# Opening of a two-layer mixer kernel: products of ones while the input is under way, first weight in halves on ScalarE's queue, blocks of x made straight from PSUM

## Chip, cores and metric

One core of one Trainium2 chip runs the program. The metric is the time of one execution on the device in microseconds (us), the median of several runs.

## What is computed

Two layers of a decoder with four mixing branches, one step for a prompt of 1024 tokens and for 8 single tokens of a second group, which share the weights. Cut to what matters here:

```python
def mixer_layer(x, ...):
    h = rms_norm(x, norm_g)                       # x / sqrt(mean(x^2) + eps) * g
    (a_b, a_c, a_h, a_gate, s_q, s_k, s_v, s_gate,
     c_u, c_v, c_gate, d_q, d_k, d_v, d_gate) = jnp.split(h @ w_in, SPLIT_POINTS, axis=-1)
    k = rope(s_k, pos); q = rope(s_q, pos)        # branch B: attention in a window of 128
    ...                                           # A: short convolution, C: mixing in chunks, D: dilated attention
    merged = sum over n of sigmoid(h @ w_merge[n]) * (branch[n] * silu(gate[n])) @ w_branch[n]
    return x + merged @ w_out
```

The model width is 1024, all arrays are fp32. The opening makes h for all 1032 tokens and the first of these products, the key columns of branch B (S_K).

## The kernel before

A product in fp32 is made of three products of a faster type (fp32r): every operand is split into hi, its rounded value, and lo, the rest, and PE (TensorE) makes hi*hi, hi*lo and lo*hi. For a weight, `w_std` loads the raw tile `wr`, ScalarE (ACT) writes `wh` (line 154) and POOL (GpSimd) subtracts it to get `wl` (line 156). Weight tiles are 128 x 8 x 128: 8 blocks of 128 rows of the model width.

The input x comes with tokens on the partitions and is needed with the width on the partitions. So the opening runs over three groups of token blocks (`GROUPS`: blocks 0 to 2 with the 8 single tokens in front, 3 to 5, 6 and 7), and in each over k = 0 to 7, the blocks of the width. For one k PE transposes the blocks of the group by products with `ident` (lines 259 and 262) into one PSUM tile, `sc` for even k and `ms` for odd k, of which there are two each. DVE (VectorE) copies it to `xT` (line 264), ACT makes `h0h` = hi of x times the norm's gain `gcol` (line 207), and the lo part `h0l` is made by DVE (line 209), or for k = 1 and 5 by ACT (`xg`, line 213) and POOL (line 214). The factor 1 / sqrt(mean) of the norm is applied later, from sums of squares (ACT, line 272, `rtok` at line 320).

Behind the opening `rope_products` multiplies S_K and then the query columns with h in three chunks of 344 tokens (`mm_cols`, lines 178, 181, 182) into `acc` tiles of PSUM, of which there are four.

A list scheduler orders the instructions of every engine; each engine runs its own list in order and waits by semaphores. A transfer is issued on the queue of the engine that the code names: SP (SyncE) for nearly all in the opening. `x` blocks 0 to 2 are loaded in two halves of their columns (`q`), blocks 3 to 7 whole, behind the first weight.

Of the kernel before, what the change touches and what calls it, by code (L numbers as in the profile page):

```python
# [7 lines left out]
F32 = mybir.dt.float32  # L8
F32R = mybir.dt.float32r
AF = mybir.ActivationFunctionType  # L10
# [3 lines left out]
P = 128  # L14
# [18 lines left out]
def kernel(ctx: ExitStack, tc: tile.TileContext, i, o, c):  # L33
# [13 lines left out]
    def slot(name, dt=F32):  # L47
        return sl.tile([P, T], dt, tag="slot", name=name)
# [43 lines left out]
    def load(dst, src, dist):  # L92
        d_ = sp.dma_start(dst, src)
        if len(marks) >= dist:
            tc.add_manual_dep(d_.ins, marks[-dist].name, nosync, reason="prefetch distance")


    ident = cp.tile([P, P], F32, name="ident")
    sp.dma_start(ident, c["ident"])
    band = cp.tile([P, 256], F32, name="band")  # L100
    blk2 = cp.tile([P, P], F32, name="blk2")
    onesm = cp.tile([P, P], F32, name="onesm")
# [46 lines left out]
    def split_w(shape, dmas):  # L149
        raw = wp.tile(list(shape), F32, tag="wr", name="wr", bufs=2)  # L150
        for sel, src in dmas:
            load(sel(raw), src, 4)
        hi = wp.tile(list(shape), F32R, tag="wh", name="wh", bufs=4)
        act.activation(hi, raw, AF.Copy)  # L154
        lo = wp.tile(list(shape), F32R, tag="wl", name="wl", bufs=4)
        pool.tensor_tensor(lo, raw, hi.bitcast(F32), op=ALU.subtract)  # L156
        return hi, lo

    def win_cols(l, c0, n):
# [2 lines left out]
    def w_std(src, kt):  # L162
        r = split_w([P, kt, P], [(lambda t: t, src)])
        copy_piece()
        return r
# [6 lines left out]
        return r  # L172

    def mm_cols(ps, w, kt, xh, xl, cs, first):
        hi, lo = w
        n = cs.stop - cs.start
        for k in range(kt):
            mm = pe.matmul(ps[:, :n], hi[:, k], xh[k][:, cs], start=(k == 0), stop=False)  # L178
            if k == 0 and first:
                mark(mm)  # L180
            pe.matmul(ps[:, :n], hi[:, k], xl[k][:, cs], start=False, stop=False)  # L181
            pe.matmul(ps[:, :n], lo[:, k], xh[k][:, cs], start=False, stop=(k == kt - 1))  # L182

    def mm_chunk(ps, w, kt, xh, xl, ch):
        mm_cols(ps, w, kt, xh, xl, slice(ch * CH, (ch + 1) * CH), kt == KT and ch == 0)
# [41 lines left out]
    def load_x(n0, n1):  # L227
        for n in range(n0, n1):
            xb = slot(f"xin{n}") if n < 5 else dec([P, T], f"xin{n}")
            sp.dma_start(xb[:, :DM], i["x_prompt"][0, n * P:(n + 1) * P, :])  # L230
            xin.append(xb)

    xs = slot("xs")[:NS, :DM]
    for q in range(2):
        fs = slice(q * DM // 2, (q + 1) * DM // 2)
        for n in range(3):
            if q == 0:
                xin.append(slot(f"xin{n}"))
            sp.dma_start(xin[n][:, fs], i["x_prompt"][0, n * P:(n + 1) * P, fs])
            if q == 0 and n == 0:  # L240
                sp.dma_start(xs, i["x_sample"].rearrange("b s d -> (b s) d"))
                sp.dma_start(gcol, i["norm_g"].rearrange("l (k p) -> p l k", p=P))
    w_first = [w_std(win_cols(0, S_K, P), KT)]
    load_x(3, 8)
    fcol = cp.tile([P, KT], F32, name="fcol")
    sp.dma_start(fcol, i["final_norm_g"].rearrange("(k p) -> p k", p=P))
# [4 lines left out]
    for n0, n1 in GROUPS:  # L251
        off = NS if n0 == 0 else 0
        cs = slice(NS + n0 * P - off, NS + n1 * P)
        w = cs.stop - cs.start
        for k in range(KT):
            ks_ = slice(k * P, (k + 1) * P)
            ps = pmisc() if k % 2 else pscore()
            if off:
                pe.transpose(ps[:, 0:NS], xs[:, ks_], ident[:NS, :NS])
            for n in range(n0, n1):  # L260
                c0 = off + (n - n0) * P
                pe.transpose(ps[:, c0:c0 + P], xin[n][:, ks_], ident)
            xt = xT0[k][:, cs]
            dve.tensor_copy(xt, ps[:, :w])
            split_x(0, k, cs, xt, (hh, hl), k % 4 != 1)
    for k in range(KT):
        act.dma_start(xres[0][k], xT0[k])
    sq0 = sm.tile([P, 9], F32, tag="sq0", name="sq0")
# [5 lines left out]
    for l in range(2):  # L274
# [27 lines left out]
            return rope(rope_products([w], [slot(name)])[0])  # L302


        w2 = w_first if l == 0 else [w_std(win_cols(l, S_K, P), KT)]
        w2.append(w_pair(l, S_Q, 0))
        kq = rope_products(w2, [slot("kB"), slot("qB0")])
        cosT, sinT = slot("cosT"), slot("sinT")
# [769 lines left out]
```

## Time and profile before

| what | value |
|---|---|
| median of 3 runs | 2444.82 us (2444.09 to 2446.32) |
| profiled execution | 2436.83 us |
| its span, first to last instruction | 2435.1 us |
| PE busy | 2407.3 us, 99% of the span |
| ACT, DVE, POOL busy | 706.4, 904.7, 846.4 us |
| PE's share of the chain that ended last | 96% |

The profiled execution is one run with its instructions recorded. Its time is 1.73 us more than its span and 7.99 us less than the median. An engine that is busy for 99% of the span leaves 27.8 us in which it stands still.

### The profile page before, as it was taken

What the parts mean: (1) busy time and instruction counts of PE and PEld (TensorE: products, weight loads), DVE (VectorE), ACT (ScalarE), POOL (GpSimd) and SP (SyncE); (2) the same over time, 40 slices, a digit from 0 to 9 for tenths busy, and PEclk for the clock granted to TensorE, in tenths of its full rate; (3) what the DMA queues carried; (4) which work ended last, traced back from release to release, by engine and by line L of the source; (5) the groups of instructions that cost most, each with busy time, mean ns of one, the idle gap of its engine ahead of it and who ended that gap; (6) DMA issues with size and microseconds to landing.
All of it is one profiled execution on the core that took longest, in us unless ns stands there. A gap on an engine that the chain in (4) does not pass through costs nothing.

```text
span 2435.1 us, 38874 instructions
## 1 busy us (share of the span) xinstructions
PE 2407.3 (99%) x15896; PEld 2295.0 (94%) x15896; DVE 904.7 (37%) x1938; ACT 706.4 (29%) x1526; POOL 846.4 (35%) x556
## 2 busy tenths in 40 slices
PE   8999999999999999999999999999999999999999
PEld 7998889889999999999999988898899999999998
DVE  4456534445322122215333554443442221222153
ACT  5234532323212121214323254323222221222243
POOL 3343225342223333444433413353323234434330
PEclk9999999999999999999999999999999999999999
DMA  7242215243321222223442423352352222212232
GB/s 239 90 140 81 81 46 182 66 129 88 106 67 56 96 63 95 66 68 119 148 146 74 143 72 80 89 160 72 90 132 73 70 91 66 93 57 69 76 98 99
DMA packets 295962, 235.82 MB, mean 97 GB/s; under 512 B 52756, under 2 KB 279696, under 8 KB 293416
## 3 DMA queue, kind: packets, MB, share of 16 engines
q1 hardware_dynamic: 267952, 206.25, 28.1%
q10 hardware_dynamic: 27832, 27.10, 3.9%
q8 instruction: 125, 2.05, 0.3%
q14 instruction: 53, 0.43, 0.1%
HBM read 192.35 MB, written 76.47 MB: 110 GB/s over the span
## 4 chain that ended last, share of the span: by engine, by line
PE 96%; DVE 1%; DMA 1%; ACT 1%; POOL 0%; SPq 0%; issue 0%; ACTq 0%; POOLq 0%; DVEq 0%
PE acc L181 27%; PE acc L178 26%; PE acc L182 26%; PE acc L367 2%; PE acc L370 2%; PE acc L371 2%; PE sc L519 2%; PE ms L541 2%; PE ms L536 2%; PE ms L681 1%; DVE ml L902 0%; PE ms L474 0%; POOL qs L291 0%; DMA qs<-dk 0%; DVE dkp L297 0%; PE sc L974 0%
## 5 line engine op out<-in xcount | busy, mean ns | idle before, releaser
L156 POOL TENSOR_TENSOR wl<-wr,wh 128x384 fp32r<-128x384 f32 (+2 forms) x228 | 467.6, 2053 | 846.1 <-ACT wh L154 742.0
L181 PE MATMUL acc<-h0l,wh 128*128 128x344 f32 x1584 | 512.8, 324 | 0.0
L181 PE MATMUL acc<-h1l,wh 128*128 128x344 f32 x1584 | 512.5, 324 | 0.0
L178 PE MATMUL acc<-h0h,wh 128*128 128x344 f32 x1584 | 511.7, 323 | 0.4 <-ACT wh L154 0.3
L178 PE MATMUL acc<-h1h,wh 128*128 128x344 f32 x1584 | 511.7, 323 | 0.1
L182 PE MATMUL acc<-h0h,wl 128*128 128x344 f32 x1584 | 511.4, 323 | 0.0
L182 PE MATMUL acc<-h1h,wl 128*128 128x344 f32 x1584 | 508.7, 321 | 0.0
L154 ACT ACTIVATE wh<-wr 128x384 fp32r<-128x384 f32 (+2 forms) x228 | 205.0, 900 | 428.3 <-PE acc L181 398.2
L937 DVE TENSOR_TENSOR th<-acc,rr 128x344 f32<-128x344 f32 x192 | 99.1, 516 | 567.5 <-PE acc L182 563.9
L181 PEld LDWEIGHTS acc<-h0l,wh 128*128 128x128 f32 x1584 | 299.6, 189 | 9.8 <-issue 8.8
L181 PEld LDWEIGHTS acc<-h1l,wh 128*128 128x128 f32 x1584 | 298.8, 189 | 9.6 <-issue 8.8
L178 PEld LDWEIGHTS acc<-h0h,wh 128*128 128x128 f32 x1584 | 299.6, 189 | 4.4 <-issue 2.0
L178 PEld LDWEIGHTS acc<-h1h,wh 128*128 128x128 f32 x1584 | 298.9, 189 | 3.7 <-issue 2.0
L182 PEld LDWEIGHTS acc<-h0h,wl 128*128 128x128 f32 x1584 | 299.2, 189 | 2.3 <-issue 1.2
L182 PEld LDWEIGHTS acc<-h1h,wl 128*128 128x128 f32 x1584 | 298.7, 189 | 2.3 <-issue 1.2
L943 POOL TENSOR_TENSOR mg<-mg,th 128x344 f32<-128x344 f32 x144 | 138.1, 959 | 309.8 <-DVE th L942 309.8
L938 ACT ACTIVATE th<-th 128x344 f32<-128x344 f32 x192 | 94.3, 491 | 518.7 <-DVE th L937 518.7
L178 PE MATMUL acc<-yh,wh 128*128 128x344 f32 x576 | 184.8, 321 | 0.0
L182 PE MATMUL acc<-yh,wl 128*128 128x344 f32 x576 | 184.8, 321 | 0.0
L181 PE MATMUL acc<-yl,wh 128*128 128x344 f32 x576 | 184.8, 321 | 0.0
L181 PE MATMUL acc<-ml,wh 128*128 128x344 f32 (+3 forms) x384 | 123.1, 322 | 0.6 <-DVE ml L902 0.5
L942 DVE SCALAR_TENSOR_TENSOR th<-th,acc 128x344 f32<-128x344 f32 x144 | 73.9, 513 | 131.5 <-PE acc L182 130.8
(280 smaller groups left out, 3350.3 us busy)
## 6 DMA issues: line engine op xcount, KB each, us to landing
wr<-in_w_merge_dram SPq DMA_DIRECT2D x64, 512.0 KB
out_dram<-in_cache_dil_kv_dram SPq DMA_DIRECT2D x128, 255.9 KB
wr<-in_w_in_dram SPq DMA_DIRECT2D x60, 512.0 KB
y<-yscr SPq DMA_DIRECT2D x18, 516.0 KB
wr<-in_w_branch_dram SPq DMA_DIRECT2D x48, 192.0 KB
wr<-in_w_in_dram SPq DMA_DIRECT2D x32, 256.0 KB
wr<-in_w_out_dram SPq DMA_DIRECT2D x16, 512.0 KB
out_dram<-in_cache_dil_kv_dram SPq DMA_DIRECT2D x16, 511.0 KB
```

The lines of the kernel that those rows point to most:

```text
L154: act.activation(hi, raw, AF.Copy)
L156: pool.tensor_tensor(lo, raw, hi.bitcast(F32), op=ALU.subtract)
L178: mm = pe.matmul(ps[:, :n], hi[:, k], xh[k][:, cs], start=(k == 0), stop=False)
L181: pe.matmul(ps[:, :n], hi[:, k], xl[k][:, cs], start=False, stop=False)
L182: pe.matmul(ps[:, :n], lo[:, k], xh[k][:, cs], start=False, stop=(k == kt - 1))
L367: mm = pe.matmul(ps[:M, :N], lh, hi[:, k % kk], start=(k == 0), stop=False)
L370: pe.matmul(ps[:M, :N], ll, hi[:, k % kk], start=False, stop=False)
L371: pe.matmul(ps[:M, :N], lh, lo[:, k % kk], start=False, stop=(k == KT - 1))
L937: dve.tensor_tensor(t, pg[:, :CH], rr[:, cs], op=ALU.mult)
L938: act.activation(t, t, AF.Tanh, scale=0.5)
L942: dve.scalar_tensor_tensor(t, t, 1.0, pp[:, :CH], op0=ALU.add, op1=ALU.mult)
L943: pool.tensor_tensor(mg[m][:, cs], mg[m][:, cs], t, op=ALU.add)
```

## The change

Five edits, all in the opening:

- `ident`, `xs` (the 8 single tokens) and `gcol` are loaded on ACT's queue in place of SP's.
- The first weight comes as two tiles of 128 x 4 x 128 on ACT's queue, right behind these, in place of one on SP's behind the six halves of x. Each half is split when its `k` is reached; `mm_cols` takes a list of two weights.
- PE multiplies `onesm`, a tile of ones, with itself into a PSUM tile that nothing reads: twelve times ahead of the data, and twice behind the transposes of each of the first four k, 20 in all.
- `split_x` reads the PSUM tile of the transposes, not `xT`. The lo part is made by DVE for every k.
- The copy to `xT` (needed later, for the residual) comes behind it, on DVE for odd k, on ACT for even k.

```diff
-    sp.dma_start(ident, c["ident"])
+    act.dma_start(ident, c["ident"])
...
         raw = wp.tile(list(shape), F32, tag="wr", name="wr", bufs=2)
         for sel, src in dmas:
             load(sel(raw), src, 4)
+        return split_r(shape, raw, pool)
+
+    def split_r(shape, raw, eng):
         hi = wp.tile(list(shape), F32R, tag="wh", name="wh", bufs=4)
         act.activation(hi, raw, AF.Copy)
         lo = wp.tile(list(shape), F32R, tag="wl", name="wl", bufs=4)
-        pool.tensor_tensor(lo, raw, hi.bitcast(F32), op=ALU.subtract)
+        eng.tensor_tensor(lo, raw, hi.bitcast(F32), op=ALU.subtract)
...
         return r
 
     def mm_cols(ps, w, kt, xh, xl, cs, first):
-        hi, lo = w
         n = cs.stop - cs.start
-        for k in range(kt):
-            mm = pe.matmul(ps[:, :n], hi[:, k], xh[k][:, cs], start=(k == 0), stop=False)
-            if k == 0 and first:
+        for k_ in range(kt):
+            (hi, lo), k = (w[k_ // 4], k_ % 4) if isinstance(w, list) else (w, k_)
+            mm = pe.matmul(ps[:, :n], hi[:, k], xh[k_][:, cs], start=(k_ == 0), stop=False)
+            if k_ == 0 and first:
                 mark(mm)
...
+
+    def busy(n):
+        for _ in range(n):
+            pe.matmul(idle[:, :P], onesm, onesm, start=True, stop=True)
+
+    idle = pacc()
+    busy(12)
     xs = slot("xs")[:NS, :DM]
+    w_first = []
     for q in range(2):
         fs = slice(q * DM // 2, (q + 1) * DM // 2)
         for n in range(3):
                 xin.append(slot(f"xin{n}"))
             sp.dma_start(xin[n][:, fs], i["x_prompt"][0, n * P:(n + 1) * P, fs])
             if q == 0 and n == 0:
-                sp.dma_start(xs, i["x_sample"].rearrange("b s d -> (b s) d"))
-                sp.dma_start(gcol, i["norm_g"].rearrange("l (k p) -> p l k", p=P))
-    w_first = [w_std(win_cols(0, S_K, P), KT)]
+                act.dma_start(xs, i["x_sample"].rearrange("b s d -> (b s) d"))
+                act.dma_start(gcol, i["norm_g"].rearrange("l (k p) -> p l k", p=P))
+        w0_ = win_cols(0, S_K, P)[:, 4 * q:4 * q + 4]
+        w_first.append(wp.tile([P, 4, P], F32, tag="wr", name="wr", bufs=2))
+        act.dma_start(w_first[q], w0_)
     load_x(3, 8)
     fcol = cp.tile([P, KT], F32, name="fcol")
     sp.dma_start(fcol, i["final_norm_g"].rearrange("(k p) -> p k", p=P))
...
             for n in range(n0, n1):
                 c0 = off + (n - n0) * P
                 pe.transpose(ps[:, c0:c0 + P], xin[n][:, ks_], ident)
+            if off and k < 4:
+                busy(2)
+            if off and k % 4 == 0:
+                w_first[k // 4] = split_r([P, 4, P], w_first[k // 4], pool)
+            split_x(0, k, cs, ps[:, :w], (hh, hl))
             xt = xT0[k][:, cs]
-            dve.tensor_copy(xt, ps[:, :w])
-            split_x(0, k, cs, xt, (hh, hl), k % 4 != 1)
+            if k % 2:
+                dve.tensor_copy(xt, ps[:, :w])
+            else:
+                act.activation(xt, ps[:, :w], AF.Copy)
     for k in range(KT):
         act.dma_start(xres[0][k], xT0[k])
     sq0 = sm.tile([P, 9], F32, tag="sq0", name="sq0")
...
             return rope(rope_products([w], [slot(name)])[0])
 
 
-        w2 = w_first if l == 0 else [w_std(win_cols(l, S_K, P), KT)]
+        w2 = [w_first] if l == 0 else [w_std(win_cols(l, S_K, P), KT)]
         w2.append(w_pair(l, S_Q, 0))
         kq = rope_products(w2, [slot("kB"), slot("qB0")])
         cosT, sinT = slot("cosT"), slot("sinT")
```

The scheduler places the rows anew. The names in the rows are those of above with a tile number. ACT, start of the program, before:

```order
L207 ACT_TABLE_LOAD
L207 ACTIVATE h0h_0_128<-xT0_0_144,gcol_93 128x392
L207 ACTIVATE h0h_1_129<-xT0_1_145,gcol_93 128x392
L213 ACTIVATE xg_167<-xT0_1_145,gcol_93 128x392
L154 ACTIVATE wh_110<-wr_108 128x1024
L207 ACTIVATE h0h_2_130<-xT0_2_146,gcol_93 128x392
L207 ACTIVATE h0h_3_131<-xT0_3_147,gcol_93 128x392
L207 ACTIVATE h0h_4_132<-xT0_4_148,gcol_93 128x392
L207 ACTIVATE h0h_5_133<-xT0_5_149,gcol_93 128x392
```

ACT, start of the program, with the change:

```order
L99 DMA ident_81<-const_ident_dram 128x128
L252 DMA xs_109<-in_x_sample_dram 8x1024
L253 DMA gcol_93<-in_norm_g_dram 128x16x1
L256 DMA wr_118<-in_w_in_dram 128x4x128
L256 DMA wr_123<-in_w_in_dram 128x4x128
L157 ACT_TABLE_LOAD
L157 ACTIVATE wh_170<-wr_118 128x512
L157 ACTIVATE wh_212<-wr_123 128x512
L210 ACTIVATE h0h_0_139<-sc_163,gcol_93 128x392
L285 ACTIVATE xT0_0_155<-sc_163 128x392
L210 ACTIVATE h0h_1_140<-ms_177,gcol_93 128x392
L210 ACTIVATE h0h_2_141<-sc_187,gcol_93 128x392
L285 ACTIVATE xT0_2_157<-sc_187 128x392
```

The five transfers and both casts (`wh`) stand ahead of the first `h0h`, where before only one cast stood between the second and the third; `h0h` reads `sc` or `ms` in place of `xT`, and a copy to `xT` stands behind each even one.

DVE, its first rows before:

```order
L264 COPY xT0_0_144<-sc_152 128x392
L209 SCALAR_TENSOR_TENSOR h0l_0_136<-xT0_0_144,gcol_93,h0h_0_128 128x392
L264 COPY xT0_1_145<-ms_160 128x392
L264 COPY xT0_2_146<-sc_170 128x392
L209 SCALAR_TENSOR_TENSOR h0l_2_138<-xT0_2_146,gcol_93,h0h_2_130 128x392
L264 COPY xT0_3_147<-ms_178 128x392
L209 SCALAR_TENSOR_TENSOR h0l_3_139<-xT0_3_147,gcol_93,h0h_3_131 128x392
L264 COPY xT0_4_148<-sc_186 128x392
```

and with the change:

```order
L212 SCALAR_TENSOR_TENSOR h0l_0_147<-sc_163,gcol_93,h0h_0_139 128x392
L212 SCALAR_TENSOR_TENSOR h0l_1_148<-ms_177,gcol_93,h0h_1_140 128x392
L283 COPY xT0_1_156<-ms_177 128x392
L212 SCALAR_TENSOR_TENSOR h0l_2_149<-sc_187,gcol_93,h0h_2_141 128x392
L212 SCALAR_TENSOR_TENSOR h0l_3_150<-ms_197,gcol_93,h0h_3_142 128x392
L283 COPY xT0_3_158<-ms_197 128x392
L212 SCALAR_TENSOR_TENSOR h0l_4_151<-sc_207,gcol_93,h0h_4_143 128x392
```

The copy is behind the lo part of its block, and stands there for odd blocks alone.

PE, from the start of the program, before:

```order
L259 MATMUL sc_152<-ident_81,xs_96 128x8
L262 MATMUL sc_152<-ident_81,xin0_97 128x128
L259 MATMUL ms_160<-ident_81,xs_96 128x8
L262 MATMUL ms_160<-ident_81,xin0_97 128x128
L259 MATMUL sc_170<-ident_81,xs_96 128x8
```

and with the change:

```order
L239 MATMUL acc_96<-onesm_85 128x128 x15
L272 MATMUL sc_163<-ident_81,xs_109 128x8
L275 MATMUL sc_163<-ident_81,xin0_110 128x128
L272 MATMUL ms_177<-ident_81,xs_109 128x8
L275 MATMUL ms_177<-ident_81,xin0_110 128x128
L275 MATMUL sc_163<-ident_81,xin1_114 128x128
L275 MATMUL ms_177<-ident_81,xin1_114 128x128
L239 MATMUL acc_96<-onesm_85 128x128
L272 MATMUL sc_187<-ident_81,xs_109 128x8
L275 MATMUL sc_187<-ident_81,xin0_110 128x128
L275 MATMUL sc_187<-ident_81,xin1_114 128x128
L239 MATMUL acc_96<-onesm_85 128x128 x2
```

Fifteen of the twenty products of ones stand ahead of the first transpose, one and two more between the transposes of the third block. The remaining two stand right ahead of the first product with a weight.

## Rows read from the trace of the kernel before

**Rows 1.** The page: busy time, and costliest groups; columns named in the page's text.

```profile
PE 2407.3 (99%) x15896; PEld 2295.0 (94%) x15896; DVE 904.7 (37%) x1938; ACT 706.4 (29%) x1526; POOL 846.4 (35%) x556
...
L937 DVE TENSOR_TENSOR th<-acc,rr 128x344 f32<-128x344 f32 x192 | 99.1, 516 | 567.5 <-PE acc L182 563.9
```

**Rows 2.** Waits of PE, whole program: total us, times, longest us.

```profile
PE ms L501 <- DVE dkp L297: 12.0, 4, 4.7
PE sc L259 <- DMA xs<-in_x_sample_dram: 4.4, 1, 4.4
```

**Rows 3.** Windows: busy us per engine (instructions), granted clock, DMA share, GB/s.

```profile
core 0: us, PE busy (x) PEld busy (x) DVE busy (x) ACT busy (x) POOL busy (x), PEclk, DMA share, GB/s
0.00:5.00 5.00, 0.56 (x2) 0.36 (x2) 0.07 (x1) 0.00 (x0) 0.68 (x9) 1.00 0.53 77
5.00:10.00 5.00, 4.07 (x16) 2.82 (x15) 1.11 (x3) 1.90 (x2) 0.00 (x0) 1.00 0.78 232
10.00:15.00 5.00, 3.92 (x12) 2.34 (x13) 1.03 (x3) 2.67 (x4) 1.42 (x2) 1.00 1.06 378
...
20.00:25.00 5.00, 5.00 (x29) 4.88 (x27) 3.48 (x7) 3.29 (x7) 1.03 (x1) 1.00 0.59 83
25.00:50.00 25.00, 24.98 (x169) 24.24 (x167) 16.53 (x29) 23.91 (x47) 12.70 (x8) 1.00 0.83 292
```

**Rows 4.** Timeline of PE: start, us, line, tiles, [idle before and releaser].

```profile
14.57 0.66 PE L178 MATMUL acc<-h0h,wh 128*128 128x344 f32 x1 [0.29 <-ACT wh L154]
...
17.90 0.27 PE L259 MATMUL ms<-ident,xs 8*128 8x8 f32 x1 [2.39 <-DVE xT L264]
...
19.38 0.49 PE L181 MATMUL acc<-h0l,wh 128*128 128x344 f32 x1
19.66 0.49 PE L182 MATMUL acc<-h0h,wl 128*128 128x344 f32 x1
...
23.37 0.41 PE L178 MATMUL acc<-h0h,wh 128*128 128x344 f32 x1
...
27.43 0.48 PE L178 MATMUL acc<-h0h,wh 128*128 128x344 f32 x2
```

**Rows 5.** Timeline of ACT (ScalarE).

```profile
8.80 0.62 ACT L207 ACTIVATE h0h<-xT,gcol 128x392 fp32r<-128x392 f32 x1 [2.02 <-DVE xT L264]
...
13.46 1.06 ACT L154 ACTIVATE wh<-wr 128x1024 fp32r<-128x1024 f32 x1 [1.74 <-DMA wr<-in_w_in_dram]
...
19.67 0.62 ACT L207 ACTIVATE h0h<-xT,gcol 128x392 fp32r<-128x392 f32 x1 [1.17 <-DVE xT L264]
21.46 0.62 ACT L207 ACTIVATE h0h<-xT,gcol 128x392 fp32r<-128x392 f32 x1 [1.17 <-DVE xT L264]
21.99 0.61 ACT L213 ACTIVATE xg<-xT,gcol 128x392 f32<-128x392 f32 x1
```

**Rows 6.** Timeline of DVE (VectorE).

```profile
15.06 2.30 DVE L209 SCALAR_TENSOR_TENSOR h0l<-xT,gcol,h0h 128x392 fp32r<-128x392 f32 x1 [4.04 <-ACT h0h L207]
...
20.33 0.63 DVE L209 SCALAR_TENSOR_TENSOR h0l<-xT,gcol,h0h 128x392 fp32r<-128x392 f32 x1 [0.69 <-ACT h0h L207]
20.87 0.56 DVE L264 COPY xT<-ms 128x392 f32<-128x392 f32 x1
```

**Rows 7.** Timeline of SP's DMA queue.

```profile
2.60 3.53 SPq L239 DMA_DIRECT2D xin<-in_x_prompt_dram  x5
6.18 0.43 SPq L93 DMA_DIRECT2D wr<-in_w_in_dram  x1
```

**Rows 8.** Chain of waits: one product of ones with data, two instructions.

```profile
59.91 0.22 PE ms L328 x2
```

**Rows 9.** Timeline of PE around two waits for dkp.

```profile
436.25 0.63 PE L501 MATMUL ms<-ident,dkp 128*128 128x128 f32 x4 [1.58 <-DVE dkp L297]
...
525.18 1.97 PE L501 MATMUL ms<-ident,dkp 128*128 128x128 f32 x8 [4.72 <-DVE dkp L297]
```

**Rows 10.** Windows behind those two waits; columns as in Rows 3.

```profile
436.00:440.00 4.00, 3.75 (x25) 3.76 (x26) 3.45 (x3) 0.86 (x2) 3.39 (x2) 1.00 0.58 127
...
524.80:528.20 3.40, 3.02 (x13) 3.02 (x14) 3.40 (x3) 1.19 (x2) 2.63 (x2) 0.50 0.51 150
```

More of the change, by code (lines that the diff above doesn't have):

```diff
@@ L174, in mm_cols @@
     def mm_cols(ps, w, kt, xh, xl, cs, first):
-        hi, lo = w
         n = cs.stop - cs.start
-        for k in range(kt):
-            mm = pe.matmul(ps[:, :n], hi[:, k], xh[k][:, cs], start=(k == 0), stop=False)
-            if k == 0 and first:
+        for k_ in range(kt):
+            (hi, lo), k = (w[k_ // 4], k_ % 4) if isinstance(w, list) else (w, k_)
+            mm = pe.matmul(ps[:, :n], hi[:, k], xh[k_][:, cs], start=(k_ == 0), stop=False)
+            if k_ == 0 and first:
                 mark(mm)
-            pe.matmul(ps[:, :n], hi[:, k], xl[k][:, cs], start=False, stop=False)
-            pe.matmul(ps[:, :n], lo[:, k], xh[k][:, cs], start=False, stop=(k == kt - 1))
+            pe.matmul(ps[:, :n], hi[:, k], xl[k_][:, cs], start=False, stop=False)
+            pe.matmul(ps[:, :n], lo[:, k], xh[k_][:, cs], start=False, stop=(k_ == kt - 1))
     def mm_chunk(ps, w, kt, xh, xl, ch):
```

## Prediction

> **What bounds the kernel now.** I read the busy times first: PE works 2407.3 us of the 2435.1 us span [rows 1], so only places where PE stands still, or runs at a low clock, have anything to give. The list of PE's waits puts two groups at the top: 12.0 us for dkp in the attention of branch D, which the diff doesn't mention, and 4.4 us for the first input [rows 2]. The change is aimed at the opening, so the windows of the first 50 us come next. PE works 0.56 and 4.07 us in the first two stretches of 5 us, is full from 20 us on, and fills 24.98 of the 25 us from 25 to 50. ScalarE is filled there as well, 23.91 of 25 [rows 3]. So the opening has two parts: up to about 20 us PE waits for data, and behind that PE and ScalarE are both full.
>
> The timeline of PE gives the milestones: first product with the weight at 14.57, a stall of 2.39 us that ends at 17.90, product of the sixth block of columns (k = 5) at 23.37. Products follow each other at 0.29 us (19.38 to 19.66), and one lasts 0.49; at 27.43 two of them take 0.48 together [rows 4], and 169 instructions fill the 24.98 us behind 25, 0.148 each [rows 3]. I call the spacing there 0.16. The windows give a granted clock of 1.00 (2.4 GHz) all along [rows 3]; a spacing that halves under the same instruction speaks for 1.2 GHz until about 23 us, and I go by the spacing.
>
> What PE waits for is a ring of three engines: ScalarE's h0h starts at 19.67 and again at 21.46, DVE's h0l at 20.33, DVE's copy of the next block at 20.87 [rows 5, 6]. That is 0.66 + 0.54 + 0.59 = 1.79 us for each block.
>
> **The change, term by term.** The anchor is the last h0h of the first group (k = 5), now at 21.46 [rows 5].
>
> *When the first h0h can start.* Now it starts at 8.80 [rows 5]. In the changed order it stands behind the casts of both weight halves on ScalarE, so it needs ident, xs, gcol, four halves of x (0.262 MB each, xin0's second half goes out second) and two weight halves (0.262 MB each): 1.68 MB. At the pace of now, 77 GB/s to 5 us and 232 to 10 us, 1.545 MB are in at 10, the rest at 378 GB/s by 10.4 [rows 3]; with a cast of half of the 1.06 us row and a hand-over the first h0h is at 11.1. At 378 GB/s from 2 us on it would be 6.4 for the data and 7.5 for h0h. Between them: the five pieces of x on SP's queue took 3.53 us to issue where one issue takes 0.43 [rows 7], 1.4 us lost behind what stands ahead of them, which now goes by ScalarE's queue. That is worth one half of x more by 5 us, and I take the mean of 232 and 378, 305 GB/s, behind: (1.68 - 0.385 - 0.262) / 0.305 = 3.4, data at 8.4 and **h0h at 9.3**. Issuing five transfers costs ScalarE five times some 0.4 us, while it has nothing else to do before 5 us.
>
> *The ones.* One such product is two instructions, 0.22 us at the full clock [rows 8], so 0.43 at half of it. Fifteen stand ahead of the first transpose: from 1.0 us on at most 6.4, to 7.5. PE has 0.56 us of work before 5 us [rows 3], so the cover is the wait for x. Behind them stand, before the third half of x, three pairs of transposes and three more ones: 4.1 us at 1.2 GHz, 2.1 at 2.4. If the clock rises on the way the first block is ready at about 8.3 and the ones cost nothing; if it doesn't, at 11.6, and they cost 2.3.
>
> *The ring.* The copy leaves the ring; instead DVE makes lo, lo and a copy for two blocks, and ScalarE hi, copy, hi, each copy behind DVE's lo. One block pair goes hi to lo 0.66, lo to DVE's copy 0.54, copy to the next lo 0.47 (0.56 less overlap), lo to ScalarE's copy 0.59, copy to hi 0.53 (the step of 21.46 to 21.99): 2.8 us against 3.58 now [rows 5, 6]. Two prices are not in the trace. ScalarE's copy from PSUM lies between DVE's 0.56 and ScalarE's own 0.62 [rows 5, 6]; both give this step. DVE's lo from PSUM lies between 0.52, the mean of 192 DVE instructions that read an accumulator [rows 1], and the 2.30 of the one stretched h0l [rows 6]; the nearest row by shape is the 0.63 of the same instruction, taken. Stretched once for each weight half it would cost 2 x 1.7 = 3.4. The k = 5 h0h is two pairs and 1.8 behind the first: 9.3 + 7.4 = 16.7, **4.8 earlier**.
>
> *What ScalarE pays later.* It gets twelve copies and loses six xg products. Behind the anchor that is nine copies against five xg, four instructions of 0.53: **2.1 us more** on an engine that is full to 50 us. POOL loses six subtractions; it was not what PE waited for. ScalarE's idle time behind the anchor, 1.1 us in 25 to 50 and some 0.5 before [rows 3], could take up to 1.6 of it, new hand-overs can eat that, so I leave it out of the sum.
>
> Sum: 4.8 - 2.1 = 2.7 us. PE could give 6.0 (product of k = 5 at 16.7 + 0.66 against 23.37), so 3.3 us of its lead should come back as short waits for ScalarE before 55 us. The profiled execution took 2436.83, so 2434.1. It lies 7.99 below the median of the three runs, 2444.82, and I take the same distance: **2442.1**.
>
> **A rule against this.** The Trainium skill, "Trainium Kernel Development and Optimization", section Key Constraints, says that DMAs issued from the SP, ACT and POOL queues run on the same 16 DMA engines and interleave, so that several issuers save only issue time. No row here shows two busy queues in the opening. By that rule the second queue brings no pace, and the sum would be that of the rival "one pipe" below.
>
> **Rivals.** *One pipe* (0.12): the DMA share is 0.78 at 232 GB/s [rows 3], and weight halves take turns with x. For it: the share is near full already. Against it: 1.06 at 378 right after. h0h at 11.1, 1.8 later: gain 0.9, 2443.9.
>
> *Both queues fill the hole* (0.15): data by 6.4, h0h at 8.3 behind the ones, and ScalarE's idle time takes 1.6 of its extra work: 21.46 - 15.7 - 0.5 = 5.3 gained, 2439.5. For it: a share of 0.53 before 5 us [rows 3].
>
> *The clock doesn't hold* (0.14, on the other side): PE stands still between ones, transposes and first product. After a wait of 4.72 us the granted clock was 0.50 though PE worked 3.02 of the next 3.40 us; after one of 1.58 it stayed at 1.00 [rows 9, 10]. I expect no single gap above 2 us, so this speaks more against it than for it. If it happens: first h0h at 11.7 (2.4 later), and a pair of blocks costs PE six products at 0.29 and two sets of transposes at 1.2, 4.2 us against the ring's 2.8. The k = 5 product starts at 11.7 + 0.7 + 2.5 x 4.2 = 22.9, 0.5 earlier than now; with ScalarE's 2.1 us the time is 1.6 longer: 2446.4. It turns to the slower side once the clock comes up later than about 2.7 us behind the forecast's.
>
> *A later wait grows* (0.10): the scheduler also moves some DVE, ScalarE and SP rows of layer 0 behind 400 us, where PE waits for dkp. Four waits take 12.0 us [rows 2], 3.0 each, and the long one brought 3.02 us of work at half clock, 1.5 lost [rows 10]. One more such wait: 2442.1 + 4.5 = 2446.6, two: 2451.1. It decides once dkp comes 2.7 us later than now in sum.
>
> **How the numbers follow.** Forecast 0.49, rivals as given. The forecast's own range is 2440.3 to 2444.3. A change of about 0.2% (4.9 us) is what a measurement of this kernel can tell from none, so forecast, one pipe, the clock and one more wait mostly count as same, 0.76. Faster, under 2439.9: two thirds of "fill the hole" (0.10) and the tail of the forecast (0.06), 0.16. Slower, above 2449.7: two more waits (0.04), or the low clock with stretched h0l (2446.4 + 3.4; 0.04), 0.08. The range reaches from "fill the hole" with 2 us more to the low clock and one more wait: 2437.5 to 2447.
>
> **What the next profile would show.** ScalarE's first h0h between 8.3 and 10.5, its sixth near 16.7, 2.8 us for a pair; ones with 0.43 falling to 0.22 us each; products 0.16 apart from the first; no stall like the 2.39; short waits of PE for ScalarE or DVE between 20 and 55 us; ScalarE full there. I am wrong if the first h0h comes after 11, if products are 0.29 apart until the second group, if h0l stays near 2.3 us, or if the wait list behind 100 us changes by more than the opening does.

## The result, and the profile after

The changed kernel takes 2459.66 us (median of 6 runs, 2451.53 to 2462.34), the kernel before, on the same chip, 2444.45 (6 runs, 2438.01 to 2447.89): ratio 1.0061, 95% interval 1.0043 to 1.0080. It is slower, outside the forecast range of 2437.5 to 2447. The profiled execution took 2453.8 us with a span of 2451.7 (before 2436.83 and 2435.1), so the two traces lie 16.6 us apart, the medians 15.2.

The list of PE's waits, after (columns as in [rows 2]):

```profile
PE ms L521 <- DVE dks L785: 9.3, 2, 5.2
PE acc L181 <- ACT h0h L210: 7.4, 1, 7.4
PE ms L521 <- DVE dkp L317: 5.6, 2, 3.9
PE ms L494 <- POOL wsT L482: 1.8, 1, 1.8
PE ms L494 <- DVE yC L488: 1.5, 1, 1.5
```

The wait for the first input is gone, but one of 7.4 us for the first h0h has come. L521 is the place that waited 12.0 us in [rows 2], and waits 14.9 now (dkp are the rotated keys of branch D, dks is DVE's copy of their first 8 columns right behind). Two waits at L494, in branch C, are new. So there are three places to explain, and the diff names only one of them.

The windows of the opening (columns as in [rows 3]):

```profile
0.00:5.00 5.00, 3.93 (x18) 3.93 (x19) 0.07 (x1) 0.00 (x0) 0.68 (x9) 1.00 0.59 170
5.00:10.00 5.00, 5.00 (x40) 4.39 (x38) 0.00 (x0) 1.28 (x1) 0.00 (x0) 1.00 1.02 264
10.00:15.00 5.00, 0.25 (x3) 0.05 (x1) 0.00 (x0) 0.00 (x0) 0.00 (x0) 0.69 1.05 396
15.00:20.00 5.00, 2.38 (x8) 1.62 (x8) 1.36 (x3) 3.19 (x6) 2.50 (x2) 0.50 0.82 198
```

The transfers are faster than before: 5 x 170 + 5 x 264 = 2.17 MB in the first 10 us, against 1.55 [rows 3]. Yet PE, DVE and ScalarE do next to nothing from 10 to 15 us: what came was not what they waited for. The timelines of ScalarE and of the two DMA queues say what came, with POOL's wl and DVE's first h0l behind them (SPq, ACTq: issue of transfers):

```profile
0.81 4.38 SPq L250 DMA_DIRECT2D xin<-in_x_prompt_dram  x6
5.24 10.73 SPq L233 DMA_DIRECT2D xin<-in_x_prompt_dram  x5
...
2.31 3.93 ACTq L256 DMA_DIRECT2D wr<-in_w_in_dram  x2
...
15.65 0.63 ACT L157 ACTIVATE wh<-wr 128x512 fp32r<-128x512 f32 x1 [8.09 <-DMA wr<-in_w_in_dram]
...
16.99 0.57 ACT L210 ACTIVATE h0h<-sc,gcol 128x392 fp32r<-128x392 f32 x1
...
18.65 0.58 ACT L210 ACTIVATE h0h<-ms,gcol 128x392 fp32r<-128x392 f32 x1
...
24.00 0.58 ACT L210 ACTIVATE h0h<-ms,gcol 128x392 fp32r<-128x392 f32 x1
...
16.42 2.50 POOL L159 TENSOR_TENSOR wl<-wr,wh 128x512 fp32r<-128x512 f32 x2 [15.07 <-ACT wh L157]
...
17.59 0.63 DVE L212 SCALAR_TENSOR_TENSOR h0l<-sc,gcol,h0h 128x392 fp32r<-128x392 f32 x1 [16.64 <-ACT h0h L210]
```

ScalarE waits 8.09 us for the first weight half; it landed at 15.6, where the whole weight was there at 13.46 before [rows 5]. SP went on, at 5.24, with the five blocks 3 to 7 of x, 2.62 MB. All that both queues had to move (ident, xs, gcol 0.11, six halves of x 1.57, weight 0.52, five blocks 2.62) is 4.82 MB; by 15 us 4.15 MB were in. The weight was issued by 6.3 us and yet wasn't all there: by the trace's records of single DMA packets its last one, 512 bytes long, ended at 15.87, when four of the five blocks had come.

PE's timeline:

```profile
1.07 5.53 PE L239 MATMUL acc<-onesm 128*128 128x128 f32 x30 [1.07 <-POOL epst L109]
...
9.64 0.61 PE L239 MATMUL acc<-onesm 128*128 128x128 f32 x4
17.61 0.66 PE L181 MATMUL acc<-h0h,wh 128*128 128x344 f32 x1 [7.37 <-ACT h0h L210]
...
22.08 0.45 PE L184 MATMUL acc<-h0l,wh 128*128 128x344 f32 x1
22.37 0.31 PE L185 MATMUL acc<-h0h,wl 128*128 128x344 f32 x1
```

The ones hold up the first transposes (6.53, where a_spw_noones below, without them, begins at 4.47), but not h0h, which waits for the weight. Behind the wait the granted clock is 0.50 (1.2 GHz), and products stand 0.29 apart until 22 us, as before the change [rows 4].

To see where the rest was lost, I followed five instructions that both kernels have: ScalarE's last eviction of cv, branch C (L414 before, L434 after); DVE's first g of the gates behind it (L693, L713); DVE's dk x cosT in branch D (L290, L310); a z of DVE 100 us later (L718, L738); DVE's last yt (L978, L998). Their starts in each profiled execution, us:

```
kernel          cv       g      dk        z       yt     ratio of medians (95%)
before       125.14  187.26  430.50   530.95  2430.32
after        129.53  197.87  442.46   547.54  2447.32   1.0061 (1.0043-1.0080)
b_count      124.46  188.76  435.20   540.34  2446.49   1.0038 (1.0023-1.0053)
a_count      130.27  194.04  440.91   547.46  2441.28   1.0034 (1.0020-1.0048)
a_count_xact 124.51  186.61  431.50   535.59  2443.87   1.0041 (1.0028-1.0054)
a_count_spw  125.82  189.22  434.63   538.94  2446.93   1.0023 (1.0011-1.0034)
a_spw_noones 123.93  186.04  430.34   534.72  2425.40   1.0002 (0.9990-1.0014)
b_ones       128.87  190.99  436.37   542.07  2444.01   1.0041 (1.0026-1.0055)
b_psum       127.96  190.07  434.24   538.75  2439.43   1.0037 (1.0024-1.0050)
b_pool8      124.34  186.45  431.81   533.47  2428.62   0.9968 (0.9954-0.9983)
n_pool8      123.27  185.38  430.98   532.31  2427.57   0.9965 (0.9952-0.9978)
s_pool8      124.17  188.56  433.13   536.13  2431.39   0.9978 (0.9967-0.9989)
a_pool8      129.13  197.40  443.01   545.74  2441.81   1.0009 (0.9999-1.0020)
a_count_pool8 129.81 191.93  438.54   541.91  2436.27   1.0005 (0.9995-1.0015)
```

After minus before: 4.4 us at cv, 10.6 at g, 12.0 at dk, 16.6 at z, 17.0 at the end. Two executions of the kernel before (b_again) differ by 0.1 to 0.2 us in the first four and 0.6 in yt. A profile is one execution, though: that of a_count_spw was the slowest of its twelve (2453.52), that of a_spw_noones the fastest (2431.98), so for the whole time the last column counts. The opening took a quarter of the loss; 6.2 us went between 125 and 187 us, 4.6 between 430 and 531.

### The profile page after: what moved, and what is told of

The parts are those of the page before. It is cut to its first block, busy times and chain, and to the rows that moved or that the text cites. A ratio compares the mean times of both kernels' runs of the same rounds, so it can differ in the third digit from the quotient of the medians.

```text
span 2451.7 us, 38978 instructions
## 1 busy us (share of the span) xinstructions
PE 2417.5 (99%) x15936; PEld 2303.8 (94%) x15936; DVE 909.5 (37%) x1932; ACT 706.4 (29%) x1533; POOL 834.8 (34%) x551
## 3 DMA queue, kind: packets, MB, share of 16 engines
q8 instruction: 125, 2.05, 0.4%
## 4 chain that ended last, share of the span: by engine, by line
PE 94%; DMA 2%; DVE 1%; ACT 1%; issue 1%; POOL 0%; ACTq 0%; SPq 0%; POOLq 0%; DVEq 0%
PE acc L184 26%; PE acc L181 26%; PE acc L185 26%; PE sc L539 2%; PE acc L387 2%; PE acc L391 2%; PE acc L390 2%; PE ms L561 2%; PE ms L556 2%; DMA wr<-in_w_in_dram 1%; PE ms L701 1%; PE ms L494 0%; DVE ml L922 0%; POOL qs L311 0%; ACT wh L157 0%
## 5 line engine op out<-in xcount | busy, mean ns | idle before, releaser
L159 POOL TENSOR_TENSOR wl<-wr,wh 128x1024 fp32r<-128x1024 f32 (+2 forms) x229 | 465.0, 2032 | 886.0 <-ACT wh L157 802.3
L157 ACT ACTIVATE wh<-wr 128x1024 fp32r<-128x1024 f32 (+2 forms) x229 | 205.5, 898 | 447.5 <-PE acc L184 396.4
L185 PE MATMUL acc<-mh,wl 128*128 128x344 f32 (+3 forms) x384 | 122.1, 320 | 0.0
```

What stands on the lines that cost most here:

```text
L159: eng.tensor_tensor(lo, raw, hi.bitcast(F32), op=ALU.subtract)
L185: pe.matmul(ps[:, :n], lo[:, k], xh[k_][:, cs], start=False, stop=(k_ == kt - 1))
```

## The experiments

The kernel before, run beside them on other chips, had medians of 2440.1 to 2441.4, so ratios are compared, not times. Names begin with b_ for edits of the kernel before; all others are edits of the changed kernel.

**The counter (a_count, b_count).** A function copy_piece counts weight loads; from the ninth on, each load is followed by one piece of the copies of the caches to the output, which have no reader. The changed opening no longer calls w_std for the first weight, so the count is one lower, and each piece goes out one weight load later, all through the program. By 100 us the kernel before has issued four pieces, the changed one three. The forecast had not seen this. a_count restores the count in the changed kernel, b_count lowers it in the kernel before, with nothing else changed:

```diff
-    nload = [0]
+    nload = [1]      # a_count;  in the kernel before: nload = [-1], b_count
```

> The changed kernel, with the counter of weight loads that releases the cache copies started at 1 in place of 0, as the first weight no longer counts itself. Nothing is left out. Theory 'copies late' (each cache copy goes out one weight load later than before, and one of 1 MB lands in the stage at 150 to 190 us, where branch C and the values wait for their own transfers): that copy goes out near 66 us again, PE's waits of 1.77 and 1.50 us at line 494 near 178 us are gone with the low clock behind them, and the time falls by 6 to 10 us, to about 2450 to 2454. Rival 'all from the opening' (the later waits only follow from the lag of the opening): the waits at line 494 stay, time 2457 to 2462.

> The kernel before, with the same counter started at -1, so that each cache copy goes out one weight load later; the opening is untouched. Nothing is left out. Theory 'copies late': waits of PE for the spatial weights or yC near 173 us appear, 5 to 10 us slower than before, 2450 to 2454. Rival 'all from the opening': no new wait, within 2 us of before.

a_count 2450.87, ratio 1.0034 (1.0020 to 1.0048); b_count 2453.03, 1.0038 (1.0023 to 1.0053). The intervals of a_count and of the changed kernel overlap, but from cv to g a_count loses 1.6 us where the changed kernel loses 6.2. That stretch: SP's timeline before, then the changed kernel (timelines of SP, ScalarE and PE, and a window):

```profile
151.80 0.56 SPq L93 DMA_DIRECT2D out_dram<-in_cache_dil_kv_dram  x1
...
158.61 0.69 SPq L93 DMA_DIRECT2D out_dram<-in_cache_dil_kv_dram  x1
...
162.24 0.58 SPq L93 DMA_DIRECT2D out_dram<-in_cache_dil_kv_dram  x1
...
168.65 0.47 ACT L406 ACTIVATE vn<-acc,rtok 128x256 f32<-128x256 f32 x1 [6.84 <-DMA out_dram<-in_cache_dil_kv_dram]
...
177.55 1.09 PE L494 MATMUL ms<-wsT,cv 128*64 128x128 f32 x16 [1.77 <-POOL wsT L482]
...
180.15 1.98 PE L494 MATMUL ms<-wsT,cv 128*64 128x128 f32 x16 [1.50 <-DVE yC L488]
...
180.00:185.00 5.00, 4.85 (x26) 4.52 (x27) 1.38 (x3) 0.00 (x0) 2.00 (x1) 0.50 0.45 118
```

Where the kernel before issues its fifth piece (151.80, 0.52 MB in 16 packets, the last of which ended at 158.3), the changed one issues the fourth (158.61, 0.52 MB in 8 packets, the last ended at 167.8) and then the fifth (162.24), of twice the size of the sixth that went out there. ScalarE's vn, an eviction of values, waits 6.84 us, by the profile for such a piece (4.25 us, for another transfer, in a_count); its weight casts, POOL's wsT and DVE's yC, which stand behind, are late for PE, and after the two waits PE works at a granted clock of 0.50. With the old count the wait for wsT is gone, that for yC stays (1.4). b_count shows that the count alone is enough to make the kernel before slower: PE's waits in it, whole program:

```profile
PE ms L501 <- DVE dkp L297: 17.4, 4, 6.1
...
PE ms L474 <- DVE yC L468: 1.5, 1, 1.5
```

It loses 2.2 us between cv and g (yC's wait), and 4.7 between dk and z, where its waits are for dkp (below).

**The weight (a_count_spw, a_count_xact).** Both keep the old count. In a_count_spw the weight halves go out on SP's queue behind the six halves of x and ahead of blocks 3 to 7; in a_count_xact the blocks 3 to 7 go behind the weight on ACT's queue, so that they no longer run beside it.

```diff
-        act.dma_start(w_first[q], w0_)
+        if q:
+            sp.dma_start(w_first[0], win_cols(0, S_K, P)[:, 0:4])
+            sp.dma_start(w_first[1], w0_)
...
-    load_x(3, 8)
+    load_x(3, 8, act)          # a_count_xact; the weight as in the change
```

> The changed kernel with the counter at 1, and both halves of the first weight issued on SP's queue behind the six halves of x and ahead of x blocks 3 to 7; ident, xs and gcol stay on ScalarE's queue. Nothing is left out. Theory 'weight shares the engines with x' (on its own queue the weight is served beside 2 MB of x that only later groups need): first h0h from 16.99 to between 9 and 12 us, PE's wait of 7.4 us shrinks to under 3, no half clock behind 18 us, the lag against before at 100 us falls from 4.4 to between -3 and 0, time 2440 to 2446. Rival 'the chain of hi, lo and copy makes the lag': first h0h earlier too, but the lag at 100 us stays at 3 or more, time 2448 or more.

> The changed kernel with the counter at 1, and x blocks 3 to 7 issued on ScalarE's queue behind the two weight halves in place of SP's queue; gcol with its 4-byte pieces stays ahead of the weight. Nothing is left out. Theory 'weight shares the engines with later x': the halves have the engines for themselves and land near 10 to 11 us, first h0h between 10 and 12.5 in place of 16.99. Rival 'the 4-byte pieces of gcol ahead of it on the queue hold the weight back': first h0h stays at 15 or later. Time at 100 us against before: 0 to 2 late by the theory, 4 or more by the rival.

a_count_spw 2448.15, ratio 1.0023 (1.0011 to 1.0034). Its timelines of SP, ScalarE and PE:

```profile
4.33 0.84 SPq L257 DMA_DIRECT2D wr<-in_w_in_dram  x1
...
5.78 6.11 SPq L233 DMA_DIRECT2D xin<-in_x_prompt_dram  x5
...
11.13 0.63 ACT L157 ACTIVATE wh<-wr 128x512 fp32r<-128x512 f32 x1 [7.53 <-DMA wr<-in_w_in_dram]
...
12.29 0.42 PE L181 MATMUL acc<-h0h,wh 128*128 128x344 f32 x1 [1.59 <-ACT h0h L210]
...
19.08 0.49 PE L185 MATMUL acc<-h0h,wl 128*128 128x344 f32 x1
19.37 0.49 PE L181 MATMUL acc<-h0h,wh 128*128 128x344 f32 x1
...
20.49 0.32 PE L185 MATMUL acc<-h0h,wl 128*128 128x344 f32 x1
```

The weight is cast at 11.13, 4.5 us earlier, though its issue begins 2 us later; the first product starts 5.3 us earlier, and cv 4.5 us earlier than in a_count. But the weight also no longer stands behind gcol's 2048 pieces of 4 bytes on ACT's queue. a_count_xact tells the two apart: there it stands behind gcol as in the change, without the blocks beside it, and by the packet records its last packet ended at 10.77 in place of 15.87. So the weight was late because the blocks of x ran beside it on the other queue. In a_count_xact it is cast at 13.58 all the same, as ScalarE was issuing the five blocks until 12.28 and only then loaded its function table. h0h came at 14.11, between the two expectations; cv came at 124.51, 0.6 ahead of the kernel before, as the theory had it. Moving transfers to the queue of an engine that is needed is a wait of its own.

The ratio of a_count_xact is 1.0041 (1.0028 to 1.0054), and a_count_spw missed its expected time, too: its products stay 0.29 apart until 19.4, against the expectation. But cv is only 0.7 us behind the kernel before there; of the 16.6 us at yt 12.5 are lost behind dk.

**The ones (b_ones, a_spw_noones).** b_ones is the kernel before with the 20 products of ones alone; a_spw_noones is a_count_spw without them.

```diff
+    def busy(n):
+        for _ in range(n):
+            pe.matmul(idle[:, :P], onesm, onesm, start=True, stop=True)
+
+    idle = pacc()
+    busy(12)
...
+            if off and k < 4:
+                busy(2)
```

> The kernel before with the 20 products of ones added and nothing else. Nothing is left out. Theory 'ones are free but do not carry' (they raise the clock, PE then waits for data and the clock falls again): first h0h up to 1 us later, time within 2 us of before, 2443 to 2447. Rival 'ones hold the clock': products 0.16 us apart from the first, 2 to 4 us faster. Rival 'ones are in the way': transposes start behind them, 2 us or more slower.

> The version with the counter at 1 and the weight halves on SP's queue ahead of x blocks 3 to 7, without the 20 products of ones. Nothing is left out. Theory 'ones gain nothing here, they only make the scheduler place the first products later': PE is as far at 50 us as with ones (within 1 us), first h0h between 9 and 12. Rival 'ones hold the clock': without them PE is 2 us or more behind at 50 us. The time itself hangs on the later waits: 2440 to 2452.

b_ones 2453.06, 1.0041 (1.0026 to 1.0055): slower, against my expectation of no difference. The rival "in the way" had 2 us or more, as the transposes do start at 6.02 in place of 4.44. The first product starts at 14.52 there, as before the change, and yet cv comes 3.7 us late: the scheduler orders the opening anew around the ones (one h0h in place of two ahead of the cast on ScalarE; PE now waits 1.9 us for wh, and later for wl and h0l). The other 10 us of its yt are lost behind g, mostly at dkp, where PE waits 16.3 us. a_spw_noones 2441.52, 1.0002 (0.9990 to 1.0014): the changed opening without ones, with the weight on SP's queue, costs nothing that can be measured (PE's waits for dkp are 9.3 us there in place of 12.0, which helps it). PE's timeline in it, beside the rows of a_count_spw above:

```profile
4.47 0.24 PE L268 MATMUL sc<-ident,xs 8*128 8x8 f32 x1 [4.47 <-DMA xs<-in_x_sample_dram]
...
12.29 0.66 PE L181 MATMUL acc<-h0h,wh 128*128 128x344 f32 x1 [3.35 <-ACT wh L157]
...
14.93 0.49 PE L185 MATMUL acc<-h0h,wl 128*128 128x344 f32 x1
15.21 0.49 PE L181 MATMUL acc<-h0h,wh 128*128 128x344 f32 x1
...
17.50 0.32 PE L184 MATMUL acc<-h0l,wh 128*128 128x344 f32 x1
17.66 0.32 PE L185 MATMUL acc<-h0h,wl 128*128 128x344 f32 x1
```

Both start the first product at 12.29. Without ones products stand 0.29 apart until 15.2, and the trace records the granted clock at 1.00 from 16.2 on; with ones 0.29 until 19.4, at 0.50 from 12.9 and 1.00 from 19.7 on. The ones made the transposes ahead of the wait quicker (0.11 apart in place of 0.21), and the products behind it slower.

**Parts from PSUM (b_psum).** The kernel before, with hi and lo from PSUM and the copies by DVE for odd k and ScalarE for even k, nothing else:

```diff
+            split_x(0, k, cs, ps[:, :w], (hh, hl))
             xt = xT0[k][:, cs]
-            dve.tensor_copy(xt, ps[:, :w])
-            split_x(0, k, cs, xt, (hh, hl), k % 4 != 1)
+            if k % 2:
+                dve.tensor_copy(xt, ps[:, :w])
+            else:
+                act.activation(xt, ps[:, :w], AF.Copy)
```

> The kernel before with one part of the change alone: hi and lo from PSUM, the copy behind them, on DVE for odd and ScalarE for even blocks. Queues, weight, ones as before. Nothing is left out. Theory 'the ring is shorter': 2.8 us for a pair of blocks in place of 3.58, the stall of 2.39 us at 15 to 18 us goes, lead of 0 to 3 us at 50 us, given back in part by 100 us. Rival 'ScalarE's longer list makes the lag': 1 us or more behind at 50 us.

2446.37, 1.0037 (1.0024 to 1.0050): the stall of 2.39 us of [rows 4] is gone, and cv is 2.8 us later all the same:

```profile
26.67 0.42 PE L178 MATMUL acc<-h0h,wh 128*128 128x344 f32 x1 [1.10 <-ACT wh L154]
```

The second weight's cast now stands behind copies and squares on ScalarE; PE waits 1.10 us for it, and products are 0.29 apart for 3 us behind. So ScalarE's longer list takes the gain and more, as the rival said.

**The place at L501/L521 (b_again, then the eight-column add).** Four waits there vary from kernel to kernel. Is that chance of an execution? b_again is the kernel before, unchanged:

> The kernel before once more, unchanged, for a second profile. In six profiles of other kernels PE waited 4.5 to 6.1 us for dkp or dks near 440 us, in the one of before 1.58. Theory 'the later waits depend on the execution' (they are set by how transfers happen to meet, so one profile of before is one draw): the wait near 436 us is 3 us or more in this profile, or its time differs from 2436.83 by 4 us or more with the difference in these waits. Rival 'before is regular there': wait within 0.5 us of 1.58, time within 3 us.

Its four waits are 1.59, 4.08, 1.64, 3.95 us, those before were 1.58, 4.72, 1.46, 4.27. In two executions they are the kernel's, not the execution's; "chance" fell. dkp is made by two adds of DVE, one of 8 columns and one of 1024. The rows of before at the first of the four (timelines of POOL and DVE; PE's wait there is in [rows 9]):

```profile
434.33 4.03 POOL L156 TENSOR_TENSOR wl<-wr,wh 128x1024 fp32r<-128x1024 f32 x1 [0.31 <-ACT wh L154]
...
434.05 0.17 DVE L296 TENSOR_TENSOR dkp<-dk,qs 128x8 f32<-128x8 f32 x1 [2.31 <-POOL qs L291]
434.14 1.97 DVE L297 TENSOR_TENSOR dkp<-dk,qs 128x1024 f32<-128x1024 f32 x1
```

and the changed kernel's, with PE's wait:

```profile
442.49 3.45 POOL L311 TENSOR_TENSOR qs<-qs,sinT 128x1032 f32<-128x1032 f32 x1 [7.10 <-DMA qs<-dk]
445.90 2.34 POOL L159 TENSOR_TENSOR wl<-wr,wh 128x1024 fp32r<-128x1024 f32 x1
...
445.98 2.28 DVE L316 TENSOR_TENSOR dkp<-dk,qs 128x8 f32<-128x8 f32 x1 [2.29 <-POOL qs L311]
448.19 1.98 DVE L317 TENSOR_TENSOR dkp<-dk,qs 128x1024 f32<-128x1024 f32 x1
...
450.31 1.09 PE L521 MATMUL ms<-ident,dkp 128*128 128x128 f32 x4 [5.23 <-DVE dks L785]
```

Before, POOL's wl comes 0.31 us after its qs, because ScalarE's wh is late; DVE's two adds slip in first (0.17 and 1.97 us), and POOL's wl is the one that is stretched, to 4.03. In the changed kernel wh is there in time, wl starts at once, and the add of 8 columns lasts until wl ends: 2.28 us in place of 0.17. The long add comes 2.1 us later by it; PE's wait is 3.65 us longer in all. The Trainium skill, "SBUF — State Buffer", section Who interferes with whom, states the rule: a DVE instruction with two SBUF inputs and a GpSimd instruction that reads SBUF exclude each other, and whichever issues first holds the other up for its whole length. These rows agree. DVE's h0l agrees with the page's other half, that one SBUF input does not contend: from SBUF it took 2.30 beside POOL's wl [rows 6], from PSUM 0.63 beside it (17.59, while POOL's wl runs from 16.42 to 18.92). In the ten traces with the short add on DVE it lasts 0.17 us, or 2.12 to 2.35.

If that is the mechanism, moving the short add to POOL should let the long one go first, as the short add then stands ahead of wl in POOL's own list.

```diff
-            dve.tensor_tensor(t[:, 0:NS], q[:, 0:NS], qs[:, 0:NS], op=ALU.add)
+            pool.tensor_tensor(t[:, 0:NS], q[:, 0:NS], qs[:, 0:NS], op=ALU.add)
```

b_pool8 is the kernel before with this edit; n_pool8 a_spw_noones, s_pool8 a_count_spw, a_pool8 the changed kernel, a_count_pool8 a_count with it.

> The kernel before with the same edit alone. Nothing is left out. By the theory its two long waits (4.7 near 525, 4.3 near 1722 us) fall to 2 us or less and the half clock behind them goes, 5 to 8 us faster, 2432 to 2436; the short ones near 436 and 1634 stay at 1.6. By the rival nothing changes or the short ones become long, 2440 or more.

> The version without ones and with the weight on SP's queue (2441.5 us, 1.0002 of before), with one more edit in the rope of branch D: the small add of 8 columns, which DVE makes ahead of the add of 1024, is made by POOL behind its own product. Nothing is left out. Theory 'POOL's weight subtraction gets ahead of DVE's add' (where POOL goes straight from the rope product to a subtraction of 2.34 us, DVE's small add lasts 2.29 in place of 0.17 and dkp comes 2.1 us or more later): with the small add on POOL, DVE's add of 1024 starts within 0.4 us of POOL's product, the waits near 438, 526, 1633 and 1718 us are 2 us or less, 4 to 8 us in all, time 2432 to 2437. Rival 'DVE's large add is held in the same way': DVE's add of 1024 lasts 4 us or starts 2 us late, waits of 4 us stay, time 2440 or more.

> As the first of these kernels, but with the 20 products of ones. Nothing is left out. With the later waits settled by the edit, the difference to the first is what the ones do: by 'ones gain nothing and move the first products back' 1 to 4 us slower, with a lag of about 2 us at 100 us; by 'ones hold the clock' 1 us or more faster.

> The changed kernel with nothing but the small add of the rope moved to POOL. Nothing is left out. Theory 'three causes add up' (late weight, late cache copies, and on top the draw of who comes first, POOL or DVE): the waits for dkp and dks fall to 3 us or less, and what is left against the kernel before with the same edit (2434.9) is the lag at 250 us of 10 us: 2443 to 2447. Rival 'it is all the draw': 2434 to 2438, as the kernel before with the edit.

> The same with the counter of weight loads at 1, so that the cache copies go out where they did before. Nothing is left out. Theory 'three causes add up': the lag at 250 us is 5 to 7 us in place of 10, time 2440 to 2443, 3 to 5 us under the kernel with the copies late. Rival 'the copies matter only through the draw': no difference beyond 1 us between the two.

b_pool8 2434.94, 0.9968 (0.9954 to 0.9983); n_pool8 2435.86, 0.9965 (0.9952 to 0.9978): faster than the kernel before. The timelines of POOL and DVE, and PE's waits, in n_pool8:

```profile
434.58 1.99 POOL L310 TENSOR_TENSOR dkp<-dk,qs 128x8 f32<-128x8 f32 x1
436.53 2.36 POOL L159 TENSOR_TENSOR wl<-wr,wh 128x1024 fp32r<-128x1024 f32 x1
...
434.53 1.96 DVE L311 TENSOR_TENSOR dkp<-dk,qs 128x1024 f32<-128x1024 f32 x1 [2.32 <-POOL qs L305]
...
PE ms L515 <- DVE dkp L311: 8.5, 4, 2.6
```

The short add is now the one held, on POOL, 1.99 us for 8 columns, and nobody waits for it. The four waits are 1.66 to 2.65 us there, and 1.68 to 2.65 in b_pool8. In all 24 places of the six kernels with this edit the long add lasts 1.96 to 2.05. a_pool8 2446.04, 1.0009 (0.9999 to 1.0020); a_count_pool8 2442.30, 1.0005 (0.9995 to 1.0015); both times inside what was expected. The intervals overlap, but the two ran beside each other: the old count brings 5.5 us by g and 3.7 in the median, and nine of its twelve runs lie under the lowest of the other twelve (2442.69). So late copies cost time by the end, too. The waits of a_pool8 missed the 3 us or less that was expected (PE):

```profile
448.63 1.08 PE L521 MATMUL ms<-ident,dkp 128*128 128x128 f32 x4 [4.01 <-DVE dkp L317]
```

The long add isn't held there (446.50, 1.98 us). But the transfers of qs, which it needs, took 10.2 us from their issue to DVE's dk x cosT, in b_pool8 7.8; by the packet records SP's queue moved 2.39 MB beside them in place of 1.23, with a piece of the copies of 0.52 MB in place of one of 0.26. So the late copies reach this place as well; that they cost the 2.4 us is likely, but not shown. s_pool8 2438.21, 0.9978 (0.9967 to 0.9989), with ones, lies 2.3 us above n_pool8, measured beside it: the intervals overlap, but nine of its twelve runs lie above the slowest of the other's six (2436.71), and each of the five milestones is 0.9 to 3.8 us later.

**gcol first (n_gcol1).** n_pool8 with gcol ahead of xs on ACT's queue and ident back on SP's:

```diff
-    act.dma_start(ident, c["ident"])
+    sp.dma_start(ident, c["ident"])
...
-                act.dma_start(xs, i["x_sample"].rearrange("b s d -> (b s) d"))
                 act.dma_start(gcol, i["norm_g"].rearrange("l (k p) -> p l k", p=P))
+                act.dma_start(xs, i["x_sample"].rearrange("b s d -> (b s) d"))
```

> As the first of these kernels, with ident back on SP's queue ahead of x, and gcol the first on ScalarE's queue, ahead of xs. Nothing is left out. Without ones the first h0h waited for gcol until 9.84 us on ScalarE's queue, against 5.42 when it went by SP's. Theory 'gcol behind xs and beside x is late': it lands 2 us or more earlier, first h0h at 8.5 to 9.5 in place of 11.13, 0 to 2 us faster. Rival 'pieces of 4 bytes beside x are slow wherever they stand': gcol lands at 9 or later, no gain.

2436.71, 0.9974 (0.9963 to 0.9986), no gain over n_pool8. gcol released ScalarE's table load at 5.62 in place of 9.01, but xs, now behind it, let PE begin at 6.58 in place of 4.44, and h0h started at 10.15 against 10.30.

## Why the prediction was wrong

- **When the first h0h can start** is the step that failed: 9.3 forecast, "between 7.5 and 11.1", 16.99 measured. The pace was right in sum: 0.385 + 0.262 + 5 x 0.305 MB is 2.17 MB by 10 us, as measured. The 1.68 MB were wrong. They counted what h0h needs, as if that came first; with the weight gone from SP's queue, blocks 3 to 7 followed the halves of x there, and these 2.62 MB came beside the weight. a_count_spw showed it: h0h at 11.66, 5.3 us back. The other 2.4 fit the last two halves of x, which came ahead of the weight as well: 2.20 MB are in at 10.1 by the same pace, and h0h at about 11.0 by the same steps. The rival "one pipe" had the right rule, but I priced it with the same 1.68 MB. The Trainium skill's sentence that the queues interleave on the same DMA engines ("Trainium Kernel Development and Optimization", section Key Constraints) agrees with the trace: a DMA share of 1.02 to 1.05 with both queues busy.
- **The ring** held: two pairs from 18.65 to 24.00, 2.68 us each against 2.8; lo from PSUM 0.63 as taken; the copy 0.50 against about 0.6. **What ScalarE pays later** fits in sum: sixth h0h 24.00 - 21.46 = 2.5 us late, plus the 2.1 of the forecast, makes 4.6; 4.4 were measured at cv. That may be luck: the same difference is 2.1 us in a_spw_noones (sixth h0h 18.15), but -0.3 in a_count_xact (21.12). With the right first h0h the sum would have been a loss of 4.6 us, not a gain of 2.7, and still short of the 17.0.
- **The ones** were hidden by the wait for the weight, but not free: "if the clock rises on the way" it did, and then fell in the wait for the weight. "The clock doesn't hold" named this, with no gap above 2 us expected; the gap was 7.37, and also behind 1.59 us in a_count_spw the clock stayed low for 7 us. Going by the spacing was right: the granted 1.00 of [rows 3] up to 23 us is no reading, as the clock records of that trace begin at 23.0.
- **No term for the counter.** I read the rows that move behind 100 us as the scheduler's choice. On SP's list they come from the count, which a deleted call changed: behind 100 us that list differs from before in the changed kernel and in b_count in the same 17 places, in a_count nowhere. Of the 6.2 us between cv and g a_count takes 4.6 back; b_count alone costs 2.2 there, so the late opening adds to it.
- **A later wait grows** had the right place, dkp, and a price of 4.5 us a wait that fits (4.6 between dk and z). It had a chance of 0.10 and no mechanism, so the fit of the price is partly luck. Before the change two of the four waits were short because wh came late by a few tenths of a us; any edit that shifts ScalarE's list there redraws them. That the draw is redrawn by b_ones, b_psum and b_count too was shown; which way it falls for a given edit can't be worked out from the trace of before.

Of the four signs that I had named as "wrong if", two came in full: h0h after 11 us, and more change behind 100 us (12.6 of the 17.0 us) than in the opening. One nearly came (products 0.29 apart until 22.4 us), and one did not (h0l near 2.3 us).

## What to carry to other kernels

Count, for a transfer that moves to another queue, everything that the queue it left will now send beside it, and not only the bytes that the next step needs. When a call goes away, look for what else it does: a counter of loads here moved every later copy. Where two engines exclude each other and a few tenths of a us decide who comes first, put the short instruction on the engine where nobody waits for it; that one line brought 0.3%, the whole rework of the opening, at its best, nothing that could be measured beside it (0.9965 against 0.9968).

## What the runs showed of the hardware

- The half clock outlasts the wait by microseconds: behind the 7.37 us products were 0.29 apart for 4.5 us, behind 1.59 us in a_count_spw for 7. Two kernels with the same first product at 12.29 were granted 1.00 from 16.2 on (PE not filled with ones before) and from 19.7 on (filled). Why the second is later stays open.
- Two DMA queues together moved 396 GB/s (one alone 378 [rows 3]), but not in the order of issue: weight pieces of 512 bytes, issued by 6.3 us, ended at 15.87, behind four blocks of x with rows of 4 KB, most of them issued later. Whether the size of the pieces decides the shares was not tried.
- An add of 8 columns takes 0.17 us on DVE, or 2.28 beside POOL's wl, and 1.99 on POOL beside DVE's long add.
- Issuing holds the issuing engine: five blocks of x on ACT's queue kept ScalarE from 6.52 to 12.26 us, and its function table came at 12.28 (a_count_xact).
